# Interleaving the two exact parts of the quarter products' weights in their tiles

## The chip, the cores and the metric

The kernel runs on one core of one Trainium2 chip. The metric is the device time of one execution in microseconds (us). Each kernel is run several times, and the median counts. Beside the times there is a profile of one execution: a page that sums it up, and a trace that can be asked for groups of instructions, for waits and for stretches of time.

## What is computed

The reference is a decoder trunk of two layers on 512 tokens of width 1024. Layer 0 mixes the tokens with a gated delta rule, layer 1 with attention in a sliding window, and both also attend to 256 memory tokens. Each layer ends with a feed-forward block, and it is in this block that the change lies:

```
def swiglu(h, w_gate_up, w_down):
    gu = h @ w_gate_up
    return (jax.nn.silu(gu[..., :D_FF]) * gu[..., D_FF:]) @ w_down
...
        x = x + swiglu(rms_norm(x, ln_ffn[layer]), w_gate_up[layer], w_down[layer])
```

`D_FF` is 2816, so gate and up are 2 x 22 blocks of 128 outputs in each layer. All of it is float32.

## The kernel before

**Exact parts.** The matrix engine (TensorE, PE in the profile) multiplies fast in a rounded form of float32, `float32r`. To keep the accuracy, every operand is split into two parts: `hi`, the value rounded to float32r, and `lo`, what the rounding left over. `split` (line 168) does it with two instructions: ScalarE (ACT) copies the raw value into `hi` (line 140), and VectorE (DVE) subtracts `hi` from the raw value and writes `lo` (line 153). A product of two matrices is then three matmuls for each block of 128 (`mm3`, line 198): weights' hi by activations' hi, hi by lo, lo by hi. Each of them loads its 128 x 128 weights anew (LDWEIGHTS, engine PEld in the profile) and then moves the activations past them. A row of the trace such as "g<-h,whi" is a matmul into the bank "g" with the activations "h" moving and the weights "whi" standing; the load for the next matmul can run beside the present matmul.

**Ordinary products.** `weight` (line 182) takes two tiles of the pool, tags `whi` and `wlo`, three buffers of each, and fills them with the parts of up to 1024 columns of raw weights. `part` (line 195) makes such a tile: 1024 + 128 elements for each partition. The matmuls are 512 wide, go into the banks "pj", and their weights begin at the start of the tile.

**Quarter products.** In `ffn` (line 1099) most gate and up blocks are computed in pairs by `quarters` (line 1275): a two by two block product (two blocks of outputs, the 512 tokens as two halves of 256) with seven products instead of eight, in the manner of Strassen. It needs sums of weights and sums of token halves. The sums of weights come by DMA with accumulation (lines 1286 and 1287) and from VectorE; the token sums ("T" in the trace, `token_sums`, line 1246) are made once for each layer. Each of the seven products (`product`, line 1294) takes a place for weights from a ring, splits 512 columns of raw weights (or sums) into it, and runs 4 x 3 matmuls, 256 wide, into a bank "g". There are 38 such quarters in the kernel: 9 and 10 in each layer's two halves.

**The ring.** `ring` (line 1130) hands out places for the parts of the weights, in turn. On its first call in a half it takes three `whi` and three `wlo` tiles. A place is one half of a `whi` tile (for hi) with the same half of a `wlo` tile (for lo), so there are six places. Within its half, a view begins `shift[0]` elements on; `begin` (line 1139) sets it to `P - 8`, that is 120 elements or 480 bytes, before the first product runs. After a half's quarters the down projection takes the same tiles back as ordinary weights.

**Order.** Instructions are issued in the order of the program, with a queue for each engine. A tile's readers and writers are tracked, so ScalarE's copy into a place waits until the matmuls that read the place before are done. Loads of raw weights are issued on SP's queue, the accumulating ones on GpSimd's (POOL).

Two other places of the kernel are used as rulers in the prediction. At the end of layer 1 (the `tail` blocks in `ffn`) the last down projections run in token halves, with matmuls 256 wide on ordinary weight tiles. And in layer 0 there are matmuls in plain float32 and transposes (`mm`, line 145, and `tr`, line 148), as well as an inverse of small blocks (`base_inverse`, line 774), in which VectorE and ScalarE read and write with steps: the update at line 793 works on rows of a 32 x 32 block, 128 bytes apart, and the copy at line 795 reads its columns.

Of the kernel before, what the change touches and what calls it, by code (L numbers as in the profile page):

```python
# [18 lines left out]
P = 128  # L19
T = 512  # L20
# [66 lines left out]
class Builder:  # L87
# [1011 lines left out]
    def ffn(self, fp, xp, layer, h, apool, rope=False):  # L1099
# [4 lines left out]
        acts, sums, open_pairs, places, waiting, shift, sized = [], [], [], [], [], [0], []  # L1104
# [25 lines left out]
        def ring():  # L1130

            if not places:
                for _ in range(3):
                    two = [self.part(tag) for tag in ("whi", "wlo")]
                    places.extend(tuple(x[:, i * T:(i + 1) * T + P] for x in two) for i in range(2))
            places.append(places.pop(0))
            return [x[:, shift[0]:shift[0] + T] for x in places[-1]]

        def begin(f, up, by, tag, bufs, then):

            o = [self.t(fp, [P, T], F32, tag, bufs) for _ in range(2)]
            steps = self.quarters(fp, [col(f + i, up) for i in range(2)], sums, by, o, ring)
            shift[0] = P - 8
            next(steps)
            while waiting:
                x = waiting.pop()
                self.nosync(self.fn(x, x, AF.Silu), self.held)
            end()
            next(steps)
            open_pairs.append((steps, then, o))  # L1150
            return o
# [51 lines left out]
        if tail < KD:  # L1203
# [9 lines left out]
            for t in parts:  # L1213
                acc = self.acc[:, t]
                for m in range(tail, KD):
                    ps, x = self.bank("pj")[:, :T // 2], self.x[m][:, t]
# [6 lines left out]
                    if seeded:  # L1223
                        x = ps
# [393 lines left out]
```

## Time and profile before

| | |
|---|---|
| median of 3 runs | 1130.63 us (1130.58 to 1131.49) |
| span of the profiled execution | 1129.4 us |
| TensorE matmul busy (PE) | 1119.9 us, 99% |
| weight loads busy (PEld) | 986.1 us, 87% |
| VectorE busy (DVE) | 827.6 us, 73% |
| ScalarE busy (ACT) | 634.4 us, 56% |
| mean granted TensorE clock | 0.998 |

In the rows of a group, "x" gives the number of instructions, then come the busy time in us and the mean duration of one in ns, then the engine's idle time before them and what ended it. In a timeline, a row has the start in us from the span's start, the duration in us, the engine, the line, the operation and its tiles; several alike that follow each other are merged, with their count. Matmuls are pipelined: one of 256 columns lasts 279 ns in the trace, but the next begins long before it ends. The distance from start to start is therefore what counts.

The four stretches with quarter products are 318.4 to 405.9, 477.5 to 575.3, 801.5 to 888.9 and 960.5 to 1058.9 us.

### The profile page before, as it was taken

How to read it: one execution, taken by the hardware profiler on the slowest of the kernel's cores; microseconds unless marked ns; L12 is line 12 of the kernel's file. 1: busy time of each engine (PE TensorE's matmuls, PEld its weight loads, DVE VectorE, ACT ScalarE, POOL GpSimd, SP SyncE). 2: the span in 40 equal slices, each digit the busy share in tenths (PEclk: the TensorE clock that was granted, in tenths of full speed). 3: DMA queues.
4: the chain of work that ended last, by engine and by line, in shares of the span. 5: the costliest groups of instructions: out<-in, count | busy, mean ns of one | idle time of the engine just before them, and what ended most of it. 6: DMA issues, size and time to landing. Idle time of an engine off the chain costs nothing.

```text
span 1129.4 us, 19330 instructions
## 1 busy us (share of the span) xinstructions
PE 1119.9 (99%) x7339; PEld 986.1 (87%) x7339; DVE 827.6 (73%) x1553; ACT 634.4 (56%) x1285; POOL 73.2 (6%) x91
## 2 busy tenths in 40 slices
PE   9999999999999999999999999999999999999997
PEld 8888778887899988899988887788999988999986
DVE  7676976577888975588955877839999634889643
ACT  8588664456566632366643555856666422666434
POOL 0000000000021001011000000000111000111001
PEclk9999999999999999999999999999999999999999
DMA  8344252234567536377533321116687533776232
GB/s 314 109 153 149 95 131 86 85 113 145 174 167 195 143 111 169 102 191 195 134 89 102 132 75 38 53 43 180 158 201 185 144 103 105 173 190 156 77 103 87
DMA packets 72401, 151.15 MB, mean 134 GB/s; under 512 B 16956, under 2 KB 18516, under 8 KB 72308
## 3 DMA queue, kind: packets, MB, share of 16 engines
q1 hardware_dynamic: 60884, 129.21, 36.3%
q0 software_dynamic: 11136, 20.45, 11.2%
q8 instruction: 57, 0.93, 0.3%
q14 instruction: 36, 0.29, 0.1%
q10 hardware_dynamic: 288, 0.26, 0.1%
HBM read 142.94 MB, written 6.96 MB: 133 GB/s over the span
## 4 chain that ended last, share of the span: by engine, by line
PE 96%; DVE 2%; ACT 1%; DMA 0%; issue 0%; DVEq 0%; SPq 0%; ACTq 0%
PE pj L146 46%; PE g L146 38%; PE sc L146 6%; PE qk L146 3%; PE pt L146 2%; PE pt L150 1%; PE g L150 1%; DVE big L153 1%; DVE qv L156 0%; DVE btmp L153 0%; DMA early<-in_early 0%; DVE wlo L153 0%; ACT sm L134 0%; DVE T L153 0%; DVE gcr L153 0%
## 5 line engine op out<-in xcount | busy, mean ns | idle before, releaser
L140 ACT ACTIVATE whi<-wraw 128x512 fp32r<-128x512 f32 (+3 forms) x318 | 235.3, 748 | 240.6 <-PE pj L146 164.0
L153 DVE TENSOR_TENSOR wlo<-wraw,whi 128x512 fp32r<-128x512 f32 (+3 forms) x318 | 262.8, 837 | 92.7 <-ACT whi L140 85.2
L146 PE MATMUL pj<-h,whi 128*128 128x512 f32 (+1 forms) x652 | 256.4, 395 | 0.0
L146 PE MATMUL pj<-l,whi 128*128 128x512 f32 (+1 forms) x652 | 254.4, 390 | 0.0
L146 PE MATMUL pj<-h,wlo 128*128 128x512 f32 (+1 forms) x652 | 254.0, 390 | 0.0
L146 PE MATMUL g<-T,whi 128*128 128x256 f32 x1216 | 216.8, 279 | 0.0
L146 PEld LDWEIGHTS g<-T,whi 128*128 128x128 f32 x1216 | 185.1, 188 | 1.3 <-DVE fu L156 1.3
L146 PE MATMUL g<-T,wlo 128*128 128x256 f32 x608 | 169.7, 279 | 0.0
L146 PEld LDWEIGHTS pj<-h,whi 128*128 128x128 f32 x652 | 122.4, 188 | 28.0 <-issue 4.1
L146 PEld LDWEIGHTS pj<-h,wlo 128*128 128x128 f32 x652 | 122.5, 188 | 25.4 <-issue 0.9
L146 PE MATMUL g<-l,whi 128*128 128x256 f32 (+1 forms) x500 | 144.5, 289 | 0.0
L146 PE MATMUL g<-h,whi 128*128 128x256 f32 (+1 forms) x500 | 144.4, 289 | 0.0
L146 PE MATMUL g<-h,wlo 128*128 128x256 f32 (+1 forms) x500 | 144.4, 289 | 0.0
L146 PEld LDWEIGHTS pj<-l,whi 128*128 128x128 f32 x652 | 122.6, 188 | 23.6 <-DVE l L1468 0.3
L146 PEld LDWEIGHTS g<-T,wlo 128*128 128x128 f32 x608 | 114.3, 188 | 0.0
L146 PEld LDWEIGHTS g<-h,whi 128*128 128x128 f32 x500 | 94.0, 188 | 1.9
L146 PEld LDWEIGHTS g<-l,whi 128*128 128x128 f32 x500 | 93.9, 188 | 1.9
L146 PEld LDWEIGHTS g<-h,wlo 128*128 128x128 f32 x500 | 93.9, 188 | 1.8
L1286 POOL DMA_DIRECT2D ws<-in_wgu x38 | 33.5, 881 | 733.0 <-DMA ws<-in_wgu 399.1
L140 ACT ACTIVATE whi<-ws 128x512 fp32r<-128x512 f32 x76 | 48.0, 631 | 42.0 <-PE g L146 35.6
L153 DVE TENSOR_TENSOR wlo<-ws,whi 128x512 fp32r<-128x512 f32 x76 | 52.0, 684 | 5.9 <-ACT whi L140 5.9
L1287 POOL DMA_DIRECT2D ws<-in_wgu x38 | 34.2, 900 | 196.4 <-DVE wlo L153 71.4
(421 smaller groups left out, 1683.2 us busy)
## 6 DMA issues: line engine op xcount, KB each, us to landing
wraw<-in_wgu SPq DMA_DIRECT2D x50, 512.0 KB, 4.4
ws<-in_wgu SPq DMA_DIRECT2D x76, 256.0 KB, 3.4
ws<-in_wgu POOLq DMA_DIRECT2D x76, 256.0 KB, 4.5
wraw<-in_win SPq DMA_DIRECT2D x26, 512.0 KB, 3.6
wraw<-in_wdn SPq DMA_DIRECT2D x32, 384.0 KB, 3.1
wraw<-in_wdn SPq DMA_DIRECT2D x32, 320.0 KB, 2.9
wraw<-in_wgu SPq DMA_DIRECT2D x38, 256.0 KB, 4.0
wraw<-in_wout SPq DMA_DIRECT2D x16, 512.0 KB, 3.6
```

The costliest lines, as they stand in the source:

```text
L140: self.copied = self.nc.scalar.activation(out, in_, AF.Copy, **kw).ins
L146: return self.nc.tensor.matmul(out, lhsT, rhs, start=start, stop=stop, skip_group_check=more).ins
L150: return self.nc.tensor.transpose(out, in_, self.ident[:k, :k]).ins
L153: return eng.tensor_tensor(out=out, in0=a, in1=b, op=op).ins
L1286: nc.gpsimd.dma_start(s1, a22, accum_op=ALU.add)
L1287: nc.gpsimd.dma_start(s3, a21, accum_op=ALU.add)
```

## The change

The ring now hands out whole tiles. A place is one of the six tiles, in the order whi, wlo, whi, wlo, whi, wlo, and holds both parts of 512 columns alternately: element 0 of hi, element 0 of lo, element 1 of hi, and so on, again from 120 elements into the tile. Each part is thus a view with a step of two elements, 8 bytes. ScalarE writes hi, VectorE reads hi and writes lo, and the weight loads read either part with that step. The 128 columns of a load lie in 1024 bytes instead of 512.

```diff
         def ring():
 
             if not places:
-                for _ in range(3):
-                    two = [self.part(tag) for tag in ("whi", "wlo")]
-                    places.extend(tuple(x[:, i * T:(i + 1) * T + P] for x in two) for i in range(2))
+                places.extend(self.part(tag) for _ in range(3) for tag in ("whi", "wlo"))
             places.append(places.pop(0))
-            return [x[:, shift[0]:shift[0] + T] for x in places[-1]]
+            two = places[-1][:, shift[0]:shift[0] + 2 * T].rearrange("p (n i) -> p n i", i=2)
+            return two[:, :, 0], two[:, :, 1]
```

## Prediction

> **What bounds the kernel now.** I read the page first: the shares of the engines and the chain that ended last.
>
> ```profile
> span 1129.4 us, 19330 instructions
> ...
> PE 1119.9 (99%) x7339; PEld 986.1 (87%) x7339; DVE 827.6 (73%) x1553; ACT 634.4 (56%) x1285; POOL 73.2 (6%) x91
> ...
> PE pj L146 46%; PE g L146 38%; PE sc L146 6%; PE qk L146 3%; PE pt L146 2%; PE pt L150 1%; PE g L150 1%; DVE big L153 1%; DVE qv L156 0%; DVE btmp L153 0%; DMA early<-in_early 0%; DVE wlo L153 0%; ACT sm L134 0%; DVE T L153 0%; DVE gcr L153 0%
> ```
>
> The matrix engine is never without work, and 38% of the chain is matmuls into the bank "g", where the quarter products go. So nothing is won here by removing a wait; time can only come from, or go into, the spacing of the matmuls. The groups by form count them, and the busy time by stretch shows their four stages.
>
> ```profile
> L146 PE MATMUL g<-T,whi 128*128 128x256 f32 x1216 | 216.8, 279 | 0.0
> ...
> L146 PE MATMUL g<-T,wlo 128*128 128x256 f32 x608 | 169.7, 279 | 0.0
> ...
> L146 PE MATMUL g<-l,whi 128*128 128x256 f32 x456 | 127.3, 279 | 0.0
> L146 PE MATMUL g<-h,whi 128*128 128x256 f32 x456 | 127.3, 279 | 0.0
> L146 PE MATMUL g<-h,wlo 128*128 128x256 f32 x456 | 127.3, 279 | 0.0
> ```
>
> ```profile
> sum 371.10, PE 371.10 PEld 369.48 DVE 330.49 ACT 234.81 POOL 54.18; mean PE 92.78 PEld 92.37 DVE 82.62 ACT 58.70 POOL 13.54
> ```
>
> The counts add up to 3192 matmuls with as many weight loads, and 3192 is 38 quarters of 7 products of 12. The last row sums the four stages (318.4 to 405.9, 477.5 to 575.3, 801.5 to 888.9, 960.5 to 1058.9): PE is busy all 371.1 us, the weight loads 369.5, VectorE 89% of it, ScalarE 63%. A busy time of overlapping matmuls says nothing of their rate. For that I read starts in the timeline, first of a quarter product, with one load beside it.
>
> ```profile
> 400.97 0.28 PE L146 MATMUL g<-h,whi 128*128 128x256 f32 x1
> ...
> 402.37 0.28 PE L146 MATMUL g<-h,whi 128*128 128x256 f32 x1
> ```
>
> ```profile
> 400.86 0.19 PEld L146 LDWEIGHTS g<-h,whi 128*128 128x128 f32 x1
> ```
>
> The first two rows are the first matmuls of two products that follow each other: 12 steps in 1.40 us, 116.7 ns each. The load is that of the first row's matmul and begins 0.11 us ahead of it, one step, when the matmul before it begins. So each load of 128 columns runs beside the 256 columns that the matmul ahead of it is reading. The cost to be found is what those 116.7 ns are made of.
>
> **What the 116.7 ns are made of.** Other places of the kernel run the same kind of matmul with other widths and addresses. Two are rows of the same end stage, with weights that start at the start of their tiles; the last two are plain float32 matmuls, which the chip does in two instructions each.
>
> ```profile
> 1090.74 0.39 PE L146 MATMUL pj<-h,whi 128*128 128x512 f32 x1
> ...
> 1103.44 0.39 PE L146 MATMUL pj<-ac10h,wlo 128*128 128x512 f32 x1
> 1103.66 0.28 PE L146 MATMUL pj<-h,whi 128*128 128x256 f32 x1
> ...
> 1105.82 0.28 PE L146 MATMUL pj<-h,whi 128*128 128x256 f32 x1
> ```
>
> ```profile
> 89.91 1.84 PE L146 MATMUL g<-kn 128*128 128x128 f32 x15
> ```
>
> ```profile
> 257.42 1.02 PE L146 MATMUL g<-N,ones 128*128 128x512 f32 x2
> ```
>
> From 1090.74 to 1103.44 there are 56 steps of width 512, 226.8 ns each; from 1103.66 to 1105.82 there are 18 steps of width 256, 120.0 ns each. The difference, 106.8 ns, is what 256 columns cost, if what comes on top of them is the same at both widths. So a matmul has 13.2 ns on top of its columns in the end stage, and 9.9 ns in the quarter products. Between these two stands only an address: the views of the quarter products' places begin 120 elements, 480 bytes, into their tiles (line 1143), the end stage's weights at the start of theirs. The tiles themselves lie at multiples of 64 bytes in the program of before, so the shifted weights stand half of 64 bytes away from the moving operand, the others stand level with it. An address alone changes the spacing by 3.3 ns; I read that as the load and the moving operand getting in each other's way in the memory.
>
> Plain float32 is the second witness; its durations (smallest, median, largest) and those of two loads:
>
> ```profile
> L146 PE MATMUL g<-N,ones x12: 592/594/697, 239.1 to 260.5; 128*128 128x512 f32 x12
> L146 PE MATMUL g<-kn x48: 270/275/275, 89.9 to 97.0; 128*128 128x128 f32 x48
> L146 PEld LDWEIGHTS pt<-pf,vt 128*64 128x64 f32 x168 | 9.0, 137 | 2.1 <-ACT sm L134 1.1 <-issue 1.1
> L146 PEld LDWEIGHTS g<-T,whi 128*128 128x128 f32 x1216 | 185.1, 188 | 1.3 <-DVE fu L156 1.3
> ```
>
> Fifteen instructions of width 128 take 1.84 us; less the 0.275 of the last one, that is 14 steps of 111.8 ns. Two of width 512 take 1.02 us and one alone 0.59, so they are 0.43 us apart. The 384 columns between the two widths cost 0.43 - 0.112 = 0.318 us, 0.83 ns a column, and 128 such columns 106 ns: on top there are about 5 ns, not 10 or 13. The load rows give the rate of loading: 51 ns more for 64 more columns, 0.80 ns a column. So in plain float32 the moving operand advances 4 bytes in 0.83 ns, and the load 4 bytes in 0.80: level. In the quarter products the moving operand advances 4 bytes in 106.8 / 256 = 0.42 ns, twice as fast as the load, and sweeps past it again and again. My reading is that the 5 ns are the fixed cost of a change of weights, and that the rest, about 4.9 ns here, is collisions of two readers at different speeds.
>
> **The change, part by part.** No instruction and no transfer is added, removed or moved on any queue; the step changes in three kinds of access, and with the tiles a wait.
>
> The loads. Each of the 3192 loads takes its 128 columns at steps of 8 bytes. At 0.80 ns a column it then covers 8 bytes in 0.80 ns: the speed of the moving operand, 8 bytes in 0.83. The places still begin 480 bytes into their tiles, and the four weights of a product stand 1024 bytes apart, so the half of 64 bytes between the readers stays. If the collisions come from the drift, they go, and the spacing falls to that of the level readers: 4.9 ns less, 111.8 by the nearest row. That is 4.9 ns x 3192 = 15.6 us less. The bottom is set by the tightest row of full loads, the transposes:
>
> ```profile
> 61.88 0.60 PE L150 MATMUL g<-consts,kn 128*128 128x128 f32 x4
> ```
>
> Four in 0.60 us, less the 0.27 that one of this width takes (as in the row of g<-kn), are three steps of 0.11 us; 6.7 ns x 3192 would be 21.4 us less, 1109 us, and 3 us below that if the rounding of the row hides 1 ns a step. The top: reading at a step may itself cost time. No load of this kernel has a step; the nearest rows are ScalarE's and VectorE's, over 128 bytes.
>
> ```profile
> 147.49 1.04 ACT L140 ACTIVATE whi<-wraw 128x1024 fp32r<-128x1024 f32 x1
> 148.90 2.01 ACT L140 ACTIVATE big<-big 96x1024 f32<-96x1024 f32 x1 [0.36 <-DVE big L153]
> ```
>
> ```profile
> 111.20 0.21 DVE L153 TENSOR_TENSOR big<-big,btmp 96x31 f32<-96x31 f32 x1
> ...
> 111.70 0.22 DVE L153 TENSOR_TENSOR big<-big,btmp 96x60 f32<-96x60 f32 x1
> ...
> 147.13 0.21 DVE L153 TENSOR_TENSOR big<-big,btmp 96x60 f32<-96x60 f32 x1
> ...
> 148.62 0.18 DVE L153 TENSOR_TENSOR big<-big,btmp 96x31 f32<-96x31 f32 x1
> ```
>
> ScalarE's copy of 1024 elements that it reads 128 bytes apart (line 795) takes 0.97 us longer than one in a row: 0.95 ns an element. On a load that would be 128 x 0.95 = 122 ns, and the load, 102 ns of columns and 5 of fixed cost, would set the pace at 229 ns: 112 ns x 3192 = 358 us more. VectorE's rows say when such a price is due. In the inverse of the base blocks (line 793) its update at 111.20 takes 31 single elements, 128 bytes apart, in 0.21 us, and the one at 148.62 takes 31 in a row in 0.18: about 1 ns an element. At 111.70 it takes 30 pairs, each 128 bytes from the next, in 0.22, and at 147.13 the same 60 elements in two runs in 0.21. So a reader that finds two neighbours at each place pays almost nothing. The weights 8 bytes apart are nearer to the pairs than to the single elements, and I take zero for the step. The Trainium skill says the same in its page "SBUF — State Buffer", Specifications: lines of 16 bytes, at full bandwidth from two hits on each line. At 8 bytes each line is hit twice, so by that rule too the step is free; the pairs at 111.70 agree.
>
> The split. ScalarE's rounding copy writes, and VectorE's subtraction reads and writes, 8 bytes apart: seven of each in a quarter, which lasts 84 x 116.7 ns = 9.8 us. By the pairs this costs nothing. At the price of the single elements it is 512 x 1 ns = 0.5 us for each, 3.5 us in a quarter on either engine. ScalarE, busy 63% or 6.2 us of 9.8, would end at 9.7 and still fit; VectorE, busy 89% or 8.7 us, would need 12.2 and become the bound, 2.4 us x 38 = 91 us. And if PE gets faster, VectorE's 8.7 us must fit in 84 x 111.8 ns = 9.4 us: they do, at 93%.
>
> The wait. Both parts now lie in one tile, with interleaved addresses, so the first matmul of a product may wait for VectorE's subtraction, where it needed only ScalarE's copy. Behind it the whole matmul queue would stand, and the subtraction takes 0.69 us. The cover is the ring of six places:
>
> ```profile
> 394.11 0.63 ACT L140 ACTIVATE whi<-wraw 128x512 fp32r<-128x512 f32 x1 [0.76 <-PE g L146]
> ```
>
> ```profile
> 397.57 0.69 DVE L153 TENSOR_TENSOR wlo<-ws,whi 128x512 fp32r<-128x512 f32 x1
> ```
>
> ScalarE waits for PE to free a place, and the subtraction for the product that begins at 402.37 ends at 398.26, 4.1 us before. I cost the wait at nothing; without that cover it would be 0.7 us x 266 products = 186 us. The ring keeps six places of the same bytes, in the same order of tiles, so what comes before and after it sees its tiles freed as before.
>
> The sum. The profiled execution has a span of 1129.4 us (the page's first line), and the median of the runs is 1130.63, so about 1.2 us lie around it: 1129.4 - 15.6 + 1.2 = 1115.0 us.
>
> **The rivals.** First, nothing happens: 1130.6 us. The 9.9 ns would be a fixed cost of this kind of matmul that plain float32 doesn't have, and the load would read without touching the moving operand. For it speaks that width 512 and width 256 in the end stage can carry the same 13.2 ns, though the load is beside all of the one and half of the other. Against it speaks that the address alone makes 3.3 ns. The Trainium skill is on this side: "TensorE: Matmul & The Clock Gate", Part 2, step by step, gives TensorE two independent read ports and has the next weights loaded without taking bandwidth from the running matmul. By that rule the time stays at 1130.6; the 120.0 against 116.7 ns do not agree with it fully.
>
> Second, slower: the collisions are counted by the pieces of memory that a load opens, not by the drift. A load over 1024 bytes opens twice as many as one over 512 in the same time. For it speaks that my second witness is weak in one point: in plain float32 both readers are slow, so its 5 ns may show a low demand and not level speed. The place is the same 3192 loads. If the 4.9 ns double, the time is 1130.6 + 15.6 = 1146.2; if only the worth of the shifted address goes, 3.3 ns x 3192 = 10.5 us, it is 1141.1. It decides as soon as a load disturbs the moving operand for more than the present 4.9 ns.
>
> Third, slower by much: the step has its price in spite of the pairs, on VectorE (about 1222 us) or in the loads (about 1489). For it speaks ScalarE's 2.01 us, against it the pairs.
>
> **How the numbers follow.** The forecast, faster, gets 0.57: the two witnesses, address and plain float32, point the same way, and the loads then go at the speed of the moving operand. Its own range is from 1106 (the transposes with their rounding) to 1122, half of the gain. Nothing happens gets 0.20. The second rival gets 0.16, a little more of it at 1141 than at 1146. The third gets 0.07. Range: 1106 to 1142; outside it are the third rival, about half of the second, and little else, some 0.17. A measurement of this kernel tells about 0.2%, 2.3 us, from no change. Faster by more 0.57, within 0.20, slower 0.23.
>
> **What would show it.** In the timeline of the quarter products, starts 112 ns apart instead of 116.7, so that a product's 12 take 1.34 us instead of 1.40, and the four stages together some 15 us less; 512-wide matmuls unchanged at 226.8; ScalarE's and VectorE's 512-wide splits at the durations that they have now; ScalarE still waiting for PE in the stages. Spacing at 116.7 would show the first rival, 120 or more the second; idle time of PE ended by VectorE, or much longer splits, the third. The forecast is wrong if the spacing does not fall, and its reason is wrong if the spacing falls while the time stays, because VectorE's 93% then sets the pace.

## The result, and the profile after

The changed kernel takes 1141.53 us (median of 4 runs, 1141.24 to 1141.89). Beside it the kernel before took 1130.70 us (4 runs, 1130.58 to 1131.49). The ratio is 1.0093 (1.0078 to 1.0107): slower by 10.8 us, where 1115.0 was forecast. The time lies inside the range, on the other side of the kernel before.

The page of the changed kernel, the same lines as those shown of before:

```profile
span 1139.9 us, 19339 instructions
...
PE 1130.4 (99%) x7339; PEld 997.1 (87%) x7339; DVE 830.0 (73%) x1553; ACT 644.3 (57%) x1285; POOL 73.0 (6%) x91
...
PE pj L146 46%; PE g L146 39%; PE sc L146 6%; PE qk L146 3%; PE pt L146 2%; PE pt L150 1%; PE g L150 1%; DMA early<-in_early 0%; DVE qv L156 0%; DVE big L153 0%; DVE btmp L153 0%; DVE wlo L153 0%; DVE T L153 0%; DVE gcr L153 0%; SPq L311 0%
```

The span grew by 10.5 us, and PE's busy time by the same 10.5. No other engine became the bound, and the chain is still matmuls. The spacing of the quarter products shows where it went. In the timeline of the changed kernel, the first matmul of the fourth product of the first stage and that of the sixty-first (a tile now holds both parts, so the name "wlo" of a tile says nothing of the part):

```profile
322.80 0.28 PE L146 MATMUL g<-h,wlo 128*128 128x256 f32 x1
...
404.88 0.28 PE L146 MATMUL g<-h,whi 128*128 128x256 f32 x1
```

The same two matmuls in the kernel before:

```profile
322.57 0.28 PE L146 MATMUL g<-h,whi 128*128 128x256 f32 x1
...
402.37 0.28 PE L146 MATMUL g<-h,whi 128*128 128x256 f32 x1
```

Between them lie 57 products of 12 matmuls, 684 steps: 79.80 us before, 82.08 after, 116.7 and 120.0 ns. The 3.33 ns more, times 3192, are 10.6 us: the whole difference. This reading, from product 4 to product 61 of the first stage, is used for the spacings of all runs with 256 columns below.

The groups by form of the changed kernel show the loads, the matmuls and the two splits:

```profile
L146 PEld LDWEIGHTS g<-T,whi 128*128 128x128 f32 x888 | 112.2, 196 | 0.3
...
L146 PE MATMUL g<-T,whi 128*128 128x256 f32 x888 | 118.8, 285 | 0.0
...
L140 ACT ACTIVATE whi<-wraw 128x512 fp32r<-128x512 f32 x100 | 66.5, 679 | 46.5 <-PE g L146 27.7 <-PE pj L146 15.2 <-DVE wraw L153 2.2
...
L153 DVE TENSOR_TENSOR whi<-wraw,whi 128x512 fp32r<-128x512 f32 x100 | 67.8, 690 | 10.4 <-ACT whi L140 7.5
```

A load lasts 196 ns instead of 188. A matmul lasts 285 instead of 279. VectorE's subtraction stays at 0.69 us. ScalarE's copy lasts 679 ns; before it was 627, as the group of the kernel before shows:

```profile
L140 ACT ACTIVATE whi<-wraw 128x512 fp32r<-128x512 f32 x190 | 116.8, 627 | 63.1 <-PE g L146 41.7 <-PE pj L146 14.3 <-DVE wraw L153 3.2
```

Over the four stretches of before, the changed kernel's sums:

```profile
sum 371.10, PE 371.10 PEld 368.43 DVE 324.02 ACT 235.25 POOL 54.16; mean PE 92.78 PEld 92.11 DVE 81.01 ACT 58.81 POOL 13.54
```

PE is busy all of the time, as before. So nothing waits; every step is simply longer.

### The profile page after: what moved, and what is told of

Same layout as the page of the kernel before. It is cut to its first block, busy times and chain, and to the rows that moved or that the text cites. A ratio compares the mean times of both kernels' runs of the same rounds, so it can differ in the third digit from the quotient of the medians.

```text
span 1139.9 us, 19339 instructions
## 1 busy us (share of the span) xinstructions
PE 1130.4 (99%) x7339; PEld 997.1 (87%) x7339; DVE 830.0 (73%) x1553; ACT 644.3 (57%) x1285; POOL 73.0 (6%) x91
## 4 chain that ended last, share of the span: by engine, by line
PE 97%; DVE 1%; DMA 0%; ACT 0%; issue 0%; SPq 0%; DVEq 0%; ACTq 0%
PE pj L146 46%; PE g L146 39%; PE sc L146 6%; PE qk L146 3%; PE pt L146 2%; PE pt L150 1%; PE g L150 1%; DMA early<-in_early 0%; DVE qv L156 0%; DVE big L153 0%; DVE btmp L153 0%; DVE wlo L153 0%; DVE T L153 0%; DVE gcr L153 0%; SPq L311 0%
## 5 line engine op out<-in xcount | busy, mean ns | idle before, releaser
L140 ACT ACTIVATE whi<-wraw 128x512 fp32r<-128x512 f32 (+2 forms) x228 | 185.0, 819 | 224.1 <-PE pj L146 158.7
L153 DVE TENSOR_TENSOR wlo<-wraw,whi 128x1024 fp32r<-128x1024 f32 (+2 forms) x128 | 135.2, 1059 | 80.8 <-ACT whi L140 75.9
L146 PE MATMUL g<-T,wlo 128*128 128x256 f32 x936 | 125.4, 285 | 0.0
L146 PEld LDWEIGHTS g<-T,wlo 128*128 128x128 f32 x936 | 118.3, 196 | 0.7 <-DVE fu L156 0.7
L146 PE MATMUL g<-T,whi 128*128 128x256 f32 x888 | 118.8, 285 | 0.0
L146 PEld LDWEIGHTS g<-T,whi 128*128 128x128 f32 x888 | 112.2, 196 | 0.3
L146 PE MATMUL g<-l,whi 128*128 128x256 f32 (+1 forms) x284 | 85.5, 301 | 0.0
L153 DVE TENSOR_TENSOR whi<-wraw,whi 128x512 fp32r<-128x512 f32 x100 | 67.8, 690 | 10.4 <-ACT whi L140 7.5
L140 ACT ACTIVATE wlo<-wraw 128x512 fp32r<-128x512 f32 x90 | 59.6, 678 | 18.8 <-PE g L146 17.5
L153 DVE TENSOR_TENSOR wlo<-wraw,wlo 128x512 fp32r<-128x512 f32 x90 | 60.8, 691 | 10.4 <-ACT wlo L140 7.2
L146 PE MATMUL g<-l,wlo 128*128 128x256 f32 x216 | 61.6, 285 | 0.0
```

The costliest lines, as they stand in the source:

```text
L140: self.copied = self.nc.scalar.activation(out, in_, AF.Copy, **kw).ins
L146: return self.nc.tensor.matmul(out, lhsT, rhs, start=start, stop=stop, skip_group_check=more).ins
L153: return eng.tensor_tensor(out=out, in0=a, in1=b, op=op).ins
```

## The experiments

Two theories stood against each other once the spacing was known. **M**, the memory: the readers disturb each other, and the stepped load has lost what the shifted address was worth (the second rival). **L**, the load: a load that steps by 8 bytes is itself longer and sets the pace, whatever the moving operand does.

### Address or step, loads or splits

Four kernels on one chip, the kernel before at 1131.04 us beside them. The first two undo the shift, in the kernel before and in the changed one:

```diff
-        shift[0] = P - 8
+        shift[0] = 0
```

> The kernel before, with the places' views at the start of their tiles (shift 0 instead of 120 elements); nothing else. If the address of the weights relative to the moving operand is worth 3.3 ns a load, as the end stage's rows say: starts 120.0 ns apart, 3192 x 3.3 ns = 10.6 us more, 1141.3 us. If the end stage's 120.0 ns have another reason (other tiles, another bank): 116.7 ns and 1130.7 us.

> The changed kernel, with shift 0. If the 8-byte step sets a pace of its own, at which the address no longer matters: 120.0 ns again, 1141.5 us. If the step costs 3.3 ns on top of whatever the address costs: 123.3 ns, 1152 us. If the step only turned the good address into a bad one: another address can be better, down to 116.7 ns and 1131 us.

The third gives the step to the loads alone. The host lays the columns of two neighbouring blocks of 128 alternately, the splits write in a row as before, hi and lo stay in separate tiles, and only the loads pick every second column:

```diff
-        s = slice(k * P, (k + 1) * P)
+        s = slice(k // step * step * P, (k // step + 1) * step * P)
+        wh, wl = (x[:, s].rearrange("p (n i) -> p i n", i=step)[:, k % step, :] for x in (wh, wl))
```

> The loads' part of the change alone: places, tiles and splits as before (contiguous), but the raw weights are laid out with the columns of two neighbouring blocks alternating, so that only the 3192 loads step by 8 bytes. If the step of the loads is the cause: 120.0 ns apart and loads of 196 ns as in the changed kernel, 1141.5 us, with ScalarE's copies back at 627 ns. If the cause is the strided splits or the two parts in one tile: 116.7 ns, 1130.7 us.

The fourth gives the step to the splits alone. The raw weights come permuted, and the splits spread them by 8 bytes so that they stand in order again; the loads read in a row:

```diff
-            self.split(raw, *w)
+            self.split(raw.rearrange("p (i n) -> p i n", i=2), *(x.rearrange("p (n i) -> p i n", i=2) for x in w))
```

> The splits' part alone: ScalarE writes hi, VectorE reads hi and writes lo with a step of 8 bytes, over raw weights laid out so that the places end as they were before; loads contiguous. If the loads are the cause: 116.7 ns and 1130.7 us, while ScalarE's copies take the 679 ns that they take in the changed kernel. If the strided splits disturb the matmuls: 120 ns and 1141.5 us.

Measured:

| run | time, us | ratio to before (95%) | spacing, ns |
|---|---|---|---|
| before, shift undone | 1140.82 | 1.0086 (1.0071 to 1.0101) | 120.0 |
| changed, shift undone | 1141.51 | 1.0091 (1.0076 to 1.0106) | 120.0 |
| loads step alone | 1141.52 | 1.0092 (1.0077 to 1.0107) | 120.0 |
| splits step alone | 1130.98 | 1.0000 (0.9990 to 1.0009) | 116.7 |

The two kernels with half of the change, in the timeline (the 684 steps) and in the groups by form. First the one in which the loads alone step:

```profile
322.66 0.28 PE L146 MATMUL g<-h,whi 128*128 128x256 f32 x1
...
404.74 0.28 PE L146 MATMUL g<-h,whi 128*128 128x256 f32 x1
```

```profile
L146 PEld LDWEIGHTS g<-T,whi 128*128 128x128 f32 x1216 | 192.1, 196 | 1.0 <-DVE fu L156 1.0
...
L140 ACT ACTIVATE whi<-wraw 128x512 fp32r<-128x512 f32 x190 | 118.5, 630 | 70.6 <-PE g L146 50.1 <-PE pj L146 15.3 <-DVE wraw L153 2.3
```

Then the one in which the splits alone step:

```profile
321.90 0.28 PE L146 MATMUL g<-h,whi 128*128 128x256 f32 x1
...
401.70 0.28 PE L146 MATMUL g<-h,whi 128*128 128x256 f32 x1
```

```profile
L146 PEld LDWEIGHTS g<-T,whi 128*128 128x128 f32 x1216 | 185.1, 188 | 1.3 <-DVE fu L156 1.3
...
L140 ACT ACTIVATE whi<-wraw 128x512 fp32r<-128x512 f32 x190 | 124.6, 677 | 57.2 <-PE g L146 35.1 <-PE pj L146 15.0 <-DVE wraw L153 3.3
```

The step in the loads is the whole change: 82.08 us for the stretch, loads of 196 ns, the time of the changed kernel, and with the splits in a row and the two parts in separate tiles. The splits' step costs ScalarE 50 ns each and the kernel nothing. Undoing the shift costs the kernel before 9.8 us and the changed kernel nothing, so the change and the lost shift do not add up. Both theories allow that: under M the worth of the shift is gone already, under L a load that paces at 120.0 hides it.

### The load's own pace

If the load sets the pace, a narrower matmul goes no faster. Two kernels move 192 columns and leave out the other 64 of the sums, apart from the first matmul of a group:

```diff
-                self.mm3(ps, w, j, sums[j][b], first and j == 0, j == 3, not first)
+                for n, (x, y) in enumerate(((0, 0), (0, 1), (1, 0))):
+                    c = slice(0, q if first and j + n == 0 else 192)
+                    self.last = self.mm(ps[:, c], w[x][:, j * P:(j + 1) * P], sums[j][b][y][:, c],
+                                        first and j + n == 0, j == 3 and n == 2, not first)
```

> The kernel before, in which the quarter products' matmuls move 192 instead of 256 columns, except the first of each bank's group: the other 64 columns of the sums are left out. Theory L (the load sets the pace at width 256): the spacing stays near 116.7 ns, at least at the 112 ns that a bare load takes in plain float32. Theory M (the moving operand sets it and the load's reads hold it up): 26.7 ns less for 64 columns, 90 ns, or whatever the bare load allows.

> The changed kernel with the same 192 columns and the same part of the sums left out. Theory L: the pace of the load with a step shows by itself, near 120 ns, some 3 ns over the narrow kernel before. Theory M: 93 ns, or the same floor as the narrow kernel before.

Twelve steps of 192 columns in the timeline of the narrowed kernel before, and its loads:

```profile
350.50 0.27 PE L146 MATMUL g<-h,wlo 128*128 128x192 f32 x1
...
351.84 0.28 PE L146 MATMUL g<-h,wlo 128*128 128x192 f32 x1
```

```profile
L146 PEld LDWEIGHTS g<-T,whi 128*128 128x128 f32 x1216 | 187.1, 194 | 14.5 <-DVE fu L156 11.3 <-DVE fg L156 3.2
```

The same of the narrowed changed kernel:

```profile
333.74 0.28 PE L146 MATMUL g<-h,wlo 128*128 128x192 f32 x1
...
335.18 1.00 PE L146 MATMUL g<-T,whi 128*128 128x192 f32 x7
```

```profile
L146 PEld LDWEIGHTS g<-T,whi 128*128 128x128 f32 x888 | 113.5, 201 | 4.8 <-DVE fu L156 4.8
```

Twelve steps take 1.34 us with loads in a row, 111.7 ns, and 1.44 us with stepped loads, 120.0 ns. (The mean over all neighbouring pairs of this width is 111.65 and 119.9.) So before, 256 columns kept the matmul at 116.7, above the 111.7 of its loads; after, a quarter less to move changes nothing. That is what L expects at this width: the stepped load paces at 120.0, 8.3 ns longer than a load in a row.

The times of these two, of one execution each, are 1135.15 and 1155.11 us, longer than at 256 columns. The waits of the narrowed kernel before say why:

```profile
PE g L146 <- DVE fu L156: 9.4, 5, 2.8
PE g L146 <- DVE fg L156: 3.0, 1, 3.0
```

PE waited 12.4 us for VectorE's results of the quarter products, which it never did in the kernel before, and its granted clock was 0.98 in two of the four stretches, where it had been 1.00.

A second pair moved 64 columns and left out the other 192, to make the load the bound in both by far:

```diff
-                    c = slice(0, q if first and j + n == 0 else 192)
+                    c = slice(0, q if first and j + n == 0 else 64)
```

> The kernel before with 64 instead of 256 columns in the quarter products' matmuls, except the first of each bank's group; the other 192 columns of the sums are left out. If the 111.6 ns at 192 columns are the load's own pace: the same here, 111 to 112 ns. If the moving operand still had a part in them: less, down to the 107 ns of 128 columns at 0.83 ns.

> The changed kernel with 64 columns and the same part left out. If the step makes the load itself longer: 120 ns as with 192 and with 256 columns. If the step costs through collisions with the moving operand: they last for a quarter of the time now, so about 2 ns of the 8 are left, 114 ns.

They took 1434.21 and 1436.04 us, one execution each. The granted clock is the reason. Two stretches of the first stage, first of the kernel before so narrowed, then of the changed one (length, then the busy us and instructions of PE, PEld, VectorE, ScalarE and GpSimd, then the granted clock, the DMA share and GB/s):

```profile
318.50:322.00 3.50, 3.50 (x35) 3.50 (x33) 3.46 (x6) 3.11 (x7) 0.87 (x1) 1.00 0.50 66
323.00:420.00 97.00, 97.00 (x457) 97.00 (x456) 52.18 (x90) 34.00 (x64) 10.50 (x12) 0.50 0.45 111
```

```profile
318.50:322.00 3.50, 3.50 (x33) 3.50 (x31) 3.37 (x6) 3.27 (x7) 0.87 (x1) 1.00 0.41 111
323.00:420.00 97.00, 97.00 (x457) 97.00 (x456) 51.12 (x87) 36.03 (x65) 10.48 (x12) 0.50 0.46 112
```

At the clock of 0.50 both are paced at 213 ns, and that stretch tells nothing of the step. The few us at 1.00 do. Six steps there, in the same two kernels:

```profile
318.61 0.28 PE L146 MATMUL g<-l,whi 128*128 128x64 f32 x1
...
319.28 0.28 PE L146 MATMUL g<-l,whi 128*128 128x64 f32 x1
```

```profile
318.81 0.28 PE L146 MATMUL g<-l,whi 128*128 128x64 f32 x1
...
319.52 0.28 PE L146 MATMUL g<-l,whi 128*128 128x64 f32 x1
```

They take 0.67 and 0.71 us. The mean over some 120 neighbouring pairs of this width at full clock in the four stages, without those right behind a 256-wide matmul, is 111.6 ns with loads in a row and 117.8 with stepped loads. So 64 columns go no faster than 192 when the loads are in a row: 111.6 is the load's own pace. The stepped load's own pace is 117.8, about 6 ns more. The 120.0 beside 192 and 256 columns has another 2.2 ns, which come only with more columns moving beside the load. Neither theory has the whole: most of the 8.3 ns is the load itself, and a part depends on the matmul beside it.

### Larger steps

How near is 8 bytes to the edge? Loads that step by 16 bytes (the third kernel's edit with four blocks alternating instead of two, splits in a row), and loads that step by 32 (the same edit on top of the change):

```diff
-                self.mm3(ps, w, j, sums[j][b], first and j == 0, j == 3, not first)
+                self.mm3(ps, w, j, sums[j][b], first and j == 0, j == 3, not first, 4)
```

> As in the loads' part alone, but the columns of four neighbouring blocks alternate: the 3192 loads step by 16 bytes, splits contiguous. If a load with a step is longer by a fixed amount: 120 ns and 1141.5 us again. If it pays for each 64 bytes that it opens (8 contiguous, 16 at 8 bytes, 32 at 16 bytes; 8 more cost 8 ns in the load): 13 to 16 ns more, 133 to 136 ns, about 1185 us. If it pays for each element that stands alone in its 16 bytes, as ScalarE did at 128 bytes (0.95 ns): about 230 ns and about 1490 us.

> The changed kernel over raw weights laid out in fours, so that the loads step by 32 bytes; splits at 8 bytes as in the change. Fixed amount: 120 ns and 1141.5 us. For each 64 bytes opened (64 of them): about 160 to 168 ns, about 1280 us. For each element alone in its 16 bytes: the same as at 16 bytes, about 230 ns.

At 16 bytes the time is 1502.54 us, 1.3285 times before (1.3263 to 1.3307). Its 684 steps and its loads:

```profile
326.91 0.40 PE L146 MATMUL g<-h,whi 128*128 128x256 f32 x1
...
486.51 0.40 PE L146 MATMUL g<-h,whi 128*128 128x256 f32 x1
```

```profile
L146 PEld LDWEIGHTS g<-T,whi 128*128 128x128 f32 x1216 | 342.0, 329 | 0.6 <-DVE fu L156 0.5
```

159.60 us for 684 steps are 233.3 ns, 121.6 more than the 111.7 of a load in a row: 0.95 ns for each of 128 columns. At 32 bytes, with loads of 338 ns, it is little more: 241.1 ns, 1526.55 us in one execution. So the price of single elements, which the forecast had from ScalarE's copy (0.95 ns), is due at 16 and at 32 bytes, and at 8 bytes a load pays at most 8.3 / 128 = 0.065 ns a column.

The Trainium skill, "SBUF — State Buffer", Specifications, gives lines of 16 bytes and asks for two hits on each. The edge lies where that rule puts it; that two hits are free agrees only nearly, with 6 to 8.3 ns on top of 111.7.

### Does a load disturb the matmul beside it?

In a 512-wide matmul the load is hidden. Two kernels put the step and the shift there. One lets the 384 loads of the output projections step by 8 bytes (host layout and index as in the third kernel), the other begins nearly all ordinary weights 480 bytes into their tiles. The two edits:

```diff
-        self.mm3(ps, w, k, mix[k], n == 0, n == KD - 1)
+        self.mm3(ps, w, k, mix[k], n == 0, n == KD - 1, step=2)
```

```diff
-        hi, lo = (self.part(tag, bufs, pool)[:, :n] for tag in tags)
+        at = 0 if pool else P - 8
+        hi, lo = (self.part(tag, bufs, pool)[:, at:at + n] for tag in tags)
```

> The kernel before, with its quarter products as they were; instead the output projection's 384 loads (weights of matmuls that are 512 wide) step by 8 bytes, over raw weights laid out with neighbouring blocks alternating. Theory L: the load has 226.8 ns and is hidden, so the spacing in the output projections stays at 226.8 ns and the time at 1131.0 us. Theory M: each load still holds up the moving operand; 3.3 ns more in these matmuls, about 230 ns, and 384 x 3.3 ns = 1.3 us more.

> The kernel before, with the ordinary weights too beginning 480 bytes into their tiles, so that nearly all 512-wide matmuls load weights half of 64 bytes away from the moving operand. Theory L: the load is hidden at that width, nothing changes, 226.8 ns and 1131.0 us. Theory M: the good address is worth its 3.3 ns here too, about 1950 loads, 6.5 us less: 223.5 ns and 1124.5 us.

Output projection in the kernel before, nine steps in 2.03 us:

```profile
274.79 0.39 PE L146 MATMUL pj<-mq0h,wlo 128*128 128x512 f32 x1
...
276.82 0.39 PE L146 MATMUL pj<-h,wlo 128*128 128x512 f32 x1
```

With stepped loads, nine steps in 2.10 us:

```profile
274.89 0.39 PE L146 MATMUL pj<-mq0h,wlo 128*128 128x512 f32 x1
...
276.99 0.39 PE L146 MATMUL pj<-h,wlo 128*128 128x512 f32 x1
```

With shifted weights, nine steps of another projection, also in 2.10 us:

```profile
429.61 0.39 PE L146 MATMUL pj<-h,whi 128*128 128x512 f32 x1
...
431.71 0.40 PE L146 MATMUL pj<-ac8h,whi 128*128 128x512 f32 x1
```

Either brings the spacing from 226.7 to 233.3 ns (mean of the matmuls concerned). The times are 1132.92 us (1.0016, 1.0007 to 1.0026), 1.8 us above the 1131.12 of the kernel before beside it, where 384 x 6.6 ns would be 2.5, and 1145.95 us (1.0132, 1.0115 to 1.0149), where the quarter products also went up a little, to 117.8 ns, though the edit leaves them alone; why is not shown. So a load that nothing waits for does lengthen the matmul beside it, and M is not empty. But the shift, worth 3.3 ns at 256 columns, costs 6.6 at 512. That runs against the reading of the forecast, in which the shift keeps the readers apart, and against both theories as they stood.

The Trainium skill, "TensorE: Matmul & The Clock Gate", Part 2, step by step, lets the next weights be loaded without taking bandwidth from the running matmul. These two runs do not agree: 6.6 ns more, from the load's address or step alone.

### The address in finer steps

Four more put the shift at other distances from a multiple of 64 bytes: `P - 12` (16 bytes beyond one) in the kernel before and in the changed one, `P - 4` (48) and `P - 6` (40) in the kernel before:

```diff
-        shift[0] = P - 8
+        shift[0] = P - 12
```

> The kernel before, views 464 bytes into their tiles, 16 past a multiple of 64. If only whether both readers stand in the same half of 64 bytes matters: 16 lies in the half of 0, so 120.0 ns and 1141 us. If the spacing goes gradually with the distance: between 116.7 and 120 ns, 1131 to 1141 us. If some address frees the load of the moving operand: towards its own 112 ns, 15 us less than before.

> The kernel before, views 496 bytes into their tiles, 48 past a multiple of 64. Same half as 32: 116.7 ns, 1131 us. Gradual: between 116.7 and 120 ns. A free address: towards 112 ns, 1116 us.

> The kernel before, views 488 bytes into their tiles, 40 past a multiple of 64 and in the middle of 16 bytes, so that a load opens 33 pieces of 16 bytes instead of 32. If such pieces count: at least the 116.7 ns of 32 and 48. If only the half counts: 116.7 ns and 1131 us.

> The changed kernel, views 464 bytes into their tiles. If the stepped load's pace is its own: 120.0 ns and 1141.5 us, as at 0 and 32. If the address matters to it after all: anything from 112 to 123 ns.

| loads | bytes beyond a multiple of 64 | time, us | ratio to before (95%) | spacing, ns |
|---|---|---|---|---|
| in a row | 16 | 1130.89 | 0.9998 (0.9988 to 1.0008) | 116.7 |
| in a row | 40 | 1136.18 | 1.0046 (1.0031 to 1.0061) | 118.3 |
| in a row | 48 | 1133.13 | 1.0018 (1.0009 to 1.0028) | 117.3 |
| 8-byte step | 16 | 1137.36 | 1.0056 (1.0041 to 1.0071) | 118.7 |

With 0 (120.0) and 32 (116.7) from above, the address counts, though not simply by its distance from a multiple of 64: 16 does as well as 32, and 40 and 48 worse. The stepped load also has better places, but at 16 it wins back 1.3 of its 3.3 ns. No kernel of the study is faster than the kernel before by more than can be told.

## Why the prediction was wrong

**What bounds the kernel: right.** PE stayed busy, and the time follows the spacing of the 3192 matmuls: 3.33 ns more each, 10.6 of the 10.8 us.

**The step that failed** is in the part on the loads: "If the collisions come from the drift, they go, and the spacing falls to that of the level readers". The collisions were never shown to come from drift. That a stepped load advances as fast as the moving operand won nothing at any address: the four spacings with stepped loads at 256 columns are 120.0, 120.0, 120.0 and 118.7 ns. The 111.8 of plain float32 was the wrong ruler: there a load of 128 columns stands beside a matmul of 128, and 192 and 64 columns show (111.7 and 111.6) that this is about the pace of loading 128 columns. The number that looked like a matmul without collisions was, as far as these spacings tell, the pace of a load.

**"I take zero for the step": wrong by 8.3 ns** (192 columns against 192), of which about 6 remain with 64 columns. VectorE's pairs were the nearer row, and the splits bear them out for VectorE (690 ns, as before). For the load the step is not free, and it matters because the load had little slack: 111.7 ns under a spacing of 116.7. Of the 8.3 ns the first 5.0 were hidden and 3.3 came out. The forecast never set the load's own pace against the spacing; it spoke of 102 ns of columns and 5 of fixed cost, 107, for the third rival only.

**The second rival** has the number, 1141.1 for 1141.5, in part by luck. Its mechanism was that a load disturbs the moving operand more, and its price was the lost worth of the shifted address. The narrowed kernels show something else first: the load's own pace rises from 111.6 to 117.8 ns, past the 116.7, which by these figures makes 1.1 of the 3.3 ns. The other 2.2 come only beside 192 or 256 columns, and there something like the rival's mechanism is at work, as at 512 columns with 6.6 ns. Which of the two readers holds up the other is not shown.

**Third rival:** right in its price, which comes at 16 bytes and beyond (233.3 ns and 1502.54 us; 229 and 1489 were named), and rightly not due at 8.

**Split and wait: as costed, nothing.** ScalarE's copies are 52 ns longer, 7 x 52 = 0.36 us in a quarter of 84 x 120.0 = 10.1 us, and fit. The wait for the subtraction never reached PE, and the kernel whose loads step without that wait takes the same time as the changed one.

**What the gain would have met.** At 111.8 ns VectorE's work was said to fit at 93%. In the narrowed kernel before, at 111.7 ns, PE waited 12.4 us for it. So even the right spacing would probably have returned much of the 15.6 us.

**Open.** Why a load at 8 bytes pays 6 ns by itself and 8.3 beside 192 columns, and why both step and shift cost a 512-wide matmul 6.6 ns while the shift wins 3.3 at 256. Columns alternating in groups of two or four would have told more of the first; that wasn't tried. Nor is it shown why a stepped load beside 256 columns is 1.3 ns better at 16 bytes than at 0 or 32. Whether the 120.0 ns of the unshifted load in a row is also its own pace is open too: it wasn't run narrowed.

## What to carry to other kernels

Before forecasting what a change of layout does to back-to-back matmuls, measure the pace of each partner alone: narrow the matmul until the spacing stops falling, read it where the granted clock is still full, and compare what is left with the present spacing. A load that is "hidden" with 5 ns to spare is nearly on the path. Here, with one load for each matmul of 256 columns, an 8-byte step of the weights cost 3.3 ns a matmul and a 16-byte step doubled the spacing. Slack does not make the step free: at 512 columns, where a load of 111.7 ns stands beside 226.7, the 8-byte step cost 6.6.

## What else the runs showed

An address of the weights alone moved the spacing between 116.7 and 120.0 ns at 256 columns, and between 226.7 and 233.3 at 512, in opposite senses for the same shift.

With 64 columns the granted clock fell from 1.00 to 0.50 some 4 us into the first stage, in both kernels, though PE was busy throughout by the profile; with 256 columns it stayed at 1.00.
